# RWKV's 16x16 block inverses turned by one transpose on TensorE in place of a DRAM round trip, one state step for both head pairs, and a new order of the mixers' work

## The chip, the cores and the metric

The kernel runs on one core of a Trainium2 chip. Its time is the device time of one execution in microseconds (us), as the median of several executions. The engines of the core are named as the profile names them: PE (TensorE, matmuls; PEld is its weight load), DVE (VectorE), ACT (ScalarE), POOL (GpSimd), SP (SyncE, which here only issues DMAs, in order).

## What is computed

Two decoder layers on 256 positions of 1024 channels. In each, one input projection feeds three token mixers (RetNet retention, FoX forgetting attention, RWKV-7), whose outputs are projected, merged under sigmoid gates, projected again and added to x; a SwiGLU network follows.

```python
for l in range(DEPTH):                      # 2
    h = _rmsnorm(x, mix_norm[l])
    ret_c, fox_c, rwkv_c, gate_c = jnp.split(h @ w_in[l], splits, axis=-1)
    y_ret, y_fox, y_rwkv = ...              # three mixers, 4 heads of 64 each
    merged = (gates[:, :, 0] * (y_ret @ p_ret[l]) + gates[:, :, 1] * (y_fox @ p_fox[l])
              + gates[:, :, 2] * (y_rwkv @ p_rwkv[l]))
    x = x + merged @ w_out[l]
    g, u = jnp.split(_rmsnorm(x, ffn_norm[l]) @ w_gate_up[l], 2, axis=-1)
    x = x + (jax.nn.silu(g) * u) @ w_down[l]

def step(state, inp):                       # RWKV-7, per head, over 256 positions
    r_t, w_t, k_t, v_t, a_t, b_t = inp
    sa = jnp.einsum('bhvk,bhk->bhv', state, a_t)
    state = (state * w_t[:, :, None, :] + sa[..., None] * b_t[:, :, None, :]
             + v_t[..., None] * k_t[:, :, None, :])
    return state, jnp.einsum('bhvk,bhk->bhv', state, r_t)
```

## The kernel before

The weights stream from DRAM through SP's queue in loads of mostly 1 MB (`raw`, L294). ACT rounds each half to `whi` (L304), DVE makes the rest `wlo` (L305), and PE multiplies with hi*hi, lo*hi and hi*lo, three matmuls (L321, L324, L325) of 128x256 for one f32 product. These weight matmuls (tiles `mm`, `mv`, `mqk`) are nearly all of PE's work, and everything of the mixers stands between them in small groups.

RWKV is computed in four chunks of C = 64 positions (NC = 4) for four heads, as two pairs `a` of two heads `h`. With `q` the chunk, there are NP = 8 pairs of chunk and head pair, each with two heads on the two halves of the 128 partitions. In the order of the program:

- `pgm` (L844): products of the chunk's vectors, masked into `gg` (L846). Among them is the strictly triangular 64x64 matrix whose inverse is wanted.
- `d1` (L856): its 16x16 diagonal blocks are written to DRAM by 8 DMAs; `lt` (L859) reads them back, one block to a partition (128 blocks), in two DMAs. `nn` (L868) is the part of the matrix off these blocks.
- `ptr` (L879), `pm` (L896): transposes and a product needed later.
- The loop (L903, L905): 15 steps on DVE, each a multiply (`ttmp`) and a reduction into `ti`, invert all 128 blocks at once, a block to a partition.
- `d2`: two DMAs (L909, `d<-ti` in the profile) write `ti` to DRAM, and eight (L914, `tb<-d`) read the blocks back as rows into the block-diagonal places of `tb`.
- `dn` (L919) transposes `tb` by two halves on DVE. `pn1` (L924) multiplies `nn` by `dn`, ACT copies the result to `vn`, `pn2` (L931) multiplies `vn` by `tb`; an addition (L935) gives inverses of the 32x32 blocks, `t1` (L936) transposes two of them. `px1` (L943) and `px2` (L951) make the block between them.
- `pu` (L961), `par` (L972), `pU` (L984), `py` (L993): with the inverse in `tb`, the chunks' products. Then the state goes from chunk to chunk: `pS` (L1003) and `S` (L1008), for each pair `a` by itself, and the rest of `py` (L1018). `pv` (L1036) turns the result for its projection.

FoX has logits `pl` (L1134), `exp` on ACT (L1139), the scaling by the reciprocal sum on DVE (L1143) and transposes `px` (L1147); retention has `psc`, `pyr`, and its normalization `pnr` (L431, sums per head) and `pvr` (L440, spread of the factors).

The mixers are generators. The numbers in `PACE` say how much time a part counts for when the next generator is chosen (the one with the least on its clock), and how far a piece of it is put ahead (`hp_...`); the framework's scheduler then sets each engine's order by priority and readiness. SP's order follows from the same, and a queue serves strictly in order.

## Time and profile before

| | us |
|---|---|
| median of 3 runs | 784.35 (783.7 to 785.01) |
| the profiled execution | 785.53 |
| its span | 783.5 |
| PE busy in it | 772.7 |
| DVE busy | 570.4 |
| ACT busy | 405.0 |
| POOL busy | 18.7 |

The profile shows one execution. The span goes from its first to its last instruction. Mixers of layer 0 lie at about 30 to 180 us, the feed-forward network of layer 0 at 228 to 410, and the mixers of layer 1 at 410 to 570. A row of a timeline is start and duration in us, engine, line, operation, output<-inputs, and in brackets the idle time before it with what ended it. A small f32 matmul has two records, and the duration of a matmul is its latency: the time from the start of one to the start of the next is what it takes of PE. "PEclk" is the clock that the throttle granted, with 1.00 for full.

### The profile page before, as it was taken

Reading aid. Unit: us, or ns where it says so; the run is one execution under the profiler, and the core shown is the slowest. Engines: PE = TensorE matmul, PEld = TensorE weight load, DVE = VectorE, ACT = ScalarE, POOL = GpSimd, SP = SyncE. Lnnn points to the kernel's source line nnn. Section 1 sums busy time; section 2 is a strip of 40 time slices with the busy share of each in tenths; the row PEclk is TensorE's granted clock in tenths of the full one; section 3 lists DMA queues with packets and bytes.
Section 4 is the critical chain, followed back from the end, with each engine's and each line's share of the span. In section 5 each row is a group of like instructions: output and inputs, shape, how many; then the busy total and the mean of one; then the engine's idle time right before and its main releaser. Section 6 shows DMA issues by size and latency. Waiting matters only on the chain.

```text
span 783.5 us, 16496 instructions
## 1 busy us (share of the span) xinstructions
PE 772.7 (99%) x7001; PEld 754.8 (96%) x7001; DVE 570.4 (73%) x902; ACT 405.0 (52%) x562; POOL 18.7 (2%) x53
## 2 busy tenths in 40 slices
PE   8999999999999999999999999998999999999998
PEld 7999999999999999999998999997999999999998
DVE  6987988869866666655668798976788776666442
ACT  5777445445555445444447773543456554544331
POOL 4000000010000000000020000000000000000000
PEclk9999999999999999999999999999999999999999
DMA  9646434335555555556464454444265465455650
GB/s 341 246 175 197 157 129 166 116 130 215 190 203 173 204 199 182 198 178 206 170 219 169 179 180 148 141 146 136 97 216 200 161 216 201 179 212 166 212 189 28
DMA packets 28378, 140.42 MB, mean 179 GB/s; under 512 B 7664, under 2 KB 9232, under 8 KB 13456
## 3 DMA queue, kind: packets, MB, share of 16 engines
q1 hardware_dynamic: 27872, 138.58, 50.7%
q8 instruction: 55, 0.90, 0.5%
q10 hardware_dynamic: 432, 0.79, 0.4%
q14 instruction: 19, 0.16, 0.1%
HBM read 136.97 MB, written 1.33 MB: 177 GB/s over the span
## 4 chain that ended last, share of the span: by engine, by line
PE 95%; DMA 2%; DVE 1%; ACT 1%; SPq 0%; issue 0%; ACTq 0%; DVEq 0%
PE mm L325 26%; PE mm L321 26%; PE mm L324 26%; PE mm L382 3%; PE mv L515 1%; PE mv L517 1%; PE mv L516 1%; PE mqk L517 1%; PE mqk L516 1%; PE mqk L515 1%; DMA raw<-in_win 1%; PE pl L1134 1%; DMA d<-ti 1%; PE px L1147 0%; PE pu L961 0%; PE ptr L879 0%
## 5 line engine op out<-in xcount | busy, mean ns | idle before, releaser
L304 ACT CAST whi<-raw 128x1024 fp32r<-128x1024 f32 (+3 forms) x258 | 264.7, 1030 | 295.1 <-PE mm L324 209.2
L305 DVE TENSOR_TENSOR wlo<-raw,whi 128x1024 fp32r<-128x1024 f32 (+3 forms) x258 | 308.6, 1198 | 134.2 <-ACT whi L304 133.4
L321 PE MATMUL mm<-xh,whi 128*128 128x256 f32 x1248 | 347.8, 279 | 0.0
L324 PE MATMUL mm<-xl,whi 128*128 128x256 f32 x1200 | 333.5, 278 | 0.0
L325 PE MATMUL mm<-xh,wlo 128*128 128x256 f32 x1200 | 333.3, 278 | 0.0
L321 PEld LDWEIGHTS mm<-xh,whi 128*128 128x128 f32 x1248 | 234.6, 188 | 0.4
L324 PEld LDWEIGHTS mm<-xl,whi 128*128 128x128 f32 x1200 | 225.4, 188 | 0.8 <-issue 0.5
L325 PEld LDWEIGHTS mm<-xh,wlo 128*128 128x128 f32 x1200 | 225.3, 188 | 0.9 <-issue 0.5
L325 PE MATMUL mm<-hi,wlo 128*128 128x256 f32 x576 | 160.0, 278 | 0.0
L324 PE MATMUL mm<-lo,whi 128*128 128x256 f32 x576 | 159.7, 277 | 0.2
L321 PE MATMUL mm<-hi,whi 128*128 128x256 f32 x576 | 159.5, 277 | 0.0
L324 PEld LDWEIGHTS mm<-lo,whi 128*128 128x128 f32 x576 | 108.4, 188 | 0.6 <-DVE lo L449 0.6
L325 PEld LDWEIGHTS mm<-hi,wlo 128*128 128x128 f32 x576 | 108.4, 188 | 0.3
L321 PEld LDWEIGHTS mm<-hi,whi 128*128 128x128 f32 x576 | 108.5, 188 | 0.0
L685 DVE TENSOR_TENSOR h<-t,mm 128x512 f32<-128x512 f32 x22 | 15.1, 686 | 9.9 <-PE mm L325 8.4
L679 DVE TENSOR_TENSOR t<-mm,rstd 128x512 f32<-128x512 f32 (+1 forms) x24 | 15.1, 644 | 7.9 <-PE mm L325 7.9
L515 PE MATMUL mv<-whi,xh 128*128 128x260 f32 (+1 forms) x64 | 18.8, 293 | 0.0
L517 PE MATMUL mv<-whi,xl 128*128 128x260 f32 (+1 forms) x64 | 18.4, 287 | 0.0
L516 PE MATMUL mv<-wlo,xh 128*128 128x260 f32 (+1 forms) x64 | 18.0, 281 | 0.0
L620 ACT ACTIVATE gate<-gate 128x512 f32<-128x512 f32 x24 | 15.1, 629 | 5.6 <-DVE gate L619 5.6
L619 DVE TENSOR_TENSOR gate<-mm,rstd 128x512 f32<-128x512 f32 x24 | 16.4, 684 | 1.1 <-PE mm L325 1.0
L628 DVE SCALAR_TENSOR_TENSOR gate<-gate,mm 128x512 f32<-128x512 f32 x24 | 15.8, 678 | 0.1
(263 smaller groups left out, 742.7 us busy)
## 6 DMA issues: line engine op xcount, KB each, us to landing
raw<-in_wg SPq DMA_DIRECT2D x44, 1024.0 KB
raw<-in_wgate SPq DMA_DIRECT2D x24, 1024.0 KB
raw<-in_wd SPq DMA_DIRECT2D x16, 1024.0 KB
raw<-in_win SPq DMA_DIRECT2D x12, 1024.0 KB
raw<-in_wo SPq DMA_DIRECT2D x8, 1024.0 KB
raw<-in_wd SPq DMA_DIRECT2D x8, 768.0 KB
raw<-in_wqk SPq DMA_DIRECT2D x4, 1024.0 KB
raw<-in_pp SPq DMA_DIRECT2D x4, 1024.0 KB
```

What stands on the lines that cost most here:

```text
L304: nc.scalar.copy(hi[:, :m * width], r)
L305: nc.vector.tensor_tensor(out=lo[:, :m * width], in0=r, in1=hi[:, :m * width].bitcast(F32), op=ALU.subtract)
L321: nc.tensor.matmul(out, wh, xh, start=first, stop=False)
L324: nc.tensor.matmul(out, wh, xl, start=False, stop=False)
L325: nc.tensor.matmul(out, wl, xh, start=False, stop=last)
L382: self.nc.tensor.matmul(ps[j][:, m, :], ws[b][i], xs[k][o], start=n == b == kk == 0, stop=n == 2 and b == 3 and kk == 3)
L515: nc.tensor.matmul(out, xh[:, s], wh, start=first, stop=False)
L516: nc.tensor.matmul(out, xh[:, s], wl, start=False, stop=False)
L517: nc.tensor.matmul(out, xl[:, s], wh, start=False, stop=last)
L619: nc.vector.tensor_tensor(out=g, in0=ps, in1=self.b2(rstd), op=ALU.mult)
L620: nc.scalar.activation(g, g, AF.Tanh, scale=0.5)
L628: nc.vector.scalar_tensor_tensor(out=g, in0=g, scalar=1.0, in1=ps, op0=ALU.add, op1=ALU.mult)
```

## The change

- `ti` has another layout: partition u*16+q holds row q of the eight blocks of chunk-and-pair u, with the blocks in the free dimension. `lt` must then hold each of the u's eight blocks on all its 16 partitions: one DMA reads 64 KB from DRAM sixteen times into 1 MB. It takes the buffer of `rav` (tag q8), so it also waits until PE has read `rav`.
- `d2` and its ten DMAs a layer are gone. One 128x128 transpose on PE (`pti`) puts the blocks' columns on the right partitions; one multiply on DVE with a constant mask (`odd`) spreads them to block-diagonal 32x32 windows (`dn`), and one stream transpose (`tw`) turns those. `pn1` has 32 columns in place of 64, `pn2` is 32 matmuls of 32x32 in place of 16 of 64x64, the addition works on `tw` at once, and ACT copies `tw` into `tb` in four pieces.
- The state step is one for both pairs: one `pS` tile of four matmuls and one addition per chunk.
- FoX's scaling by `rc` moves from DVE to ACT.
- `PACE` has new numbers, and `PINS` names 15 groups of matmuls that keep the order in which the program issues them.

```diff
+PINS = {"pU", "par", "pc", "pgm", "pl", "pm", "pn1", "pn2", "pnk", "pqk", "psc", "pss", "px1", "py", "pyf"}
-PACE = {... 'hp_merge': 44.0, 'hp_turn': 0.0, ... 'rwkv9': 15.39, ... 'rwkv23': 25.79, ...}
+PACE = {... 'hp_merge': 100.0, 'hp_turn': 68, ... 'rwkv9': 13.22, ... 'rwkv23': 12.06, ...}
-    d["tinit"] = ((p[:, None, None] // 64) * 8 + np.arange(8)[None, :, None] == np.arange(Q)[None, None, :]).astype(f)
+    d["tinit"] = np.broadcast_to(p[:, None, None] % Q == np.arange(Q)[None, None, :], (P, 8, Q)).astype(f)
+    d["odd"] = (p[:, None] // Q % 2 == np.arange(2)[None, :]).astype(f)
...
+    def pinned(self, ins):
+        if self.pend in PINS:
+            self.tc.keep_in_program_order(ins)
+        self.pend = None
+        return ins
...
-                nc.sync.dma_start(d1[b, h].rearrange("u s t -> s u t"), gg[64 * h + o:64 * h + o + Q, h::2, 2 * C + o:2 * C + o + Q])
-        lt = big.tile([P, Q, Q], F32, name="lt")
-        for g4 in range(2):
-            nc.sync.dma_start(lt[g4 * 64:(g4 + 1) * 64].rearrange("p s t -> p (s t)"), d1.rearrange("b h u s t -> (b h u) (s t)"))
+                nc.sync.dma_start(d1[:, 4 * h + b].rearrange("u s t -> s u t"), gg[64 * h + o:64 * h + o + Q, h::2, 2 * C + o:2 * C + o + Q])
+        lt = big.tile([P, 8, Q, Q], F32, tag="q8", bufs=1, name=self.nm("lt"))
+        ltf = lt.rearrange("p b s t -> p b (s t)")
+        nc.sync.dma_start(ltf.rearrange("p b x -> p (b x)"),
+                          d1.rearrange("u b s t -> u (b s t)").unsqueeze(1).broadcast_to([NP, Q, 8 * Q * Q]))
...
-        for g4 in range(2):
-            nc.sync.dma_start(d2.rearrange("b h u c j -> (b h u) c j")[:, g4 * 8:(g4 + 1) * 8, :].rearrange("q c j -> q (c j)"),
-                              ti[g4 * 64:(g4 + 1) * 64].rearrange("p c j -> p (c j)"))
-        for h in range(2):
-            for b in range(4):
-                o = b * Q
-                nc.sync.dma_start(tb[64 * h + o:64 * h + o + Q, :, h, o:o + Q], d2[b, h].rearrange("u c j -> c u j"))
...
+        px = self.ps.tile([P, NP, Q], F32, tag="sm", bufs=SM, name=self.nm("pti"))
+        self.trans(px.rearrange("p u c -> p (u c)"), ti.rearrange("p b j -> p (b j)"), idn)
+        dn = self.t2.tile([P, NP, B], F32, tag="t2", name=self.nm("dn"))
+        nc.vector.tensor_tensor(out=dn.rearrange("p u (e c) -> p u e c", e=2), in0=px.unsqueeze(2).broadcast_to([P, NP, 2, Q]),
+                                in1=c["odd"].unsqueeze(1).unsqueeze(3).broadcast_to([P, NP, 2, Q]), op=ALU.mult)
+        tw = self.t2.tile([P, NP, B], F32, tag="t2", name=self.nm("tw"))
+        nc.vector.transpose(tw, dn)
...
-            for h in range(2):
-                nc.tensor.matmul(px[hs[h], p, :], vn[hs[h], p, :], tb[hs[h], p, h, :], start=True, stop=True, tile_position=(64 * h, 64 * h))
+            for w in range(4):
+                self.mmul(px[win[w], p, :], vn[win[w], p, :], tw[win[w], p, :], start=True, stop=True, tile_position=(w * B, w * B))
...
-        for h in range(2):
-            nc.vector.tensor_tensor(out=tb[hs[h], :, h, :], in0=tb[hs[h], :, h, :], in1=px[hs[h]], op=ALU.add)
-            nc.vector.transpose(t1[lo[h]], tb[lo[h], :, h, 0:B])
+        nc.vector.tensor_tensor(out=tw, in0=tw, in1=px, op=ALU.add)
+        nc.vector.transpose(t1, tw)
+        for w in range(4):
+            o = w % 2 * B
+            nc.scalar.copy(tb[win[w], :, w // 2, o:o + B], tw[win[w]])
...
         for q in range(1, NC - 1):
+            pS = self.ps.tile([P, 2, 64], F32, tag="sm", bufs=SM, name=self.nm("pS"))
             for a in range(2):
-                pS = self.ps.tile([P, 64], F32, tag="sm", bufs=SM, name=self.nm("pS"))
...
-                ns = sm.tile([P, 64], F32, tag="S", bufs=2 * NC - 4, name=self.nm("S"))
-                nc.vector.tensor_tensor(out=ns, in0=us[:, a, q, :], in1=pS, op=ALU.add)
+            ns = sm.tile([P, 2, 64], F32, tag="S", bufs=NC - 2, name=self.nm("S"))
+            nc.vector.tensor_tensor(out=ns, in0=us[:, :, q, :], in1=pS, op=ALU.add)
...
-                nc.vector.tensor_scalar(out=lg[:, h, 0:n], in0=lg[:, h, 0:n], scalar1=rc[:, h:h + 1], scalar2=None, op0=ALU.mult)
+                nc.scalar.activation(lg[:, h, 0:n], lg[:, h, 0:n], AF.Copy, scale=rc[:, h:h + 1])
```

How the instructions stand in a row on an engine, at three places of layer 0. First SP's queue from the blocks' way out to the loads behind the inverse, before (`in_pp` and `in_wgate` are weights; x8 says eight alike):

```order
L856 DMA d_0_1325<-gg 16x8x16 x8
L294 DMA raw_1629<-in_wgate 128x2048
L859 DMA lt<-d_0_1325 64x256 x2
L294 DMA raw_1691<-in_pp 128x2048
L294 DMA raw_1856<-in_pp 128x2048
L294 DMA raw_1978<-in_wgate 128x2048
L294 DMA raw_2109<-in_wgate 128x2048
L909 DMA d_0_1326<-ti 64x128 x2
L914 DMA tb_1341<-d_0_1326 16x8x16 x8
L294 DMA raw_2197<-in_wgate 128x2048
```

and in the changed kernel:

```order
L877 DMA d_0_1325<-gg 16x8x16 x8
L880 DMA lt_1334<-d_0_1325 128x1x2048
L309 DMA raw_1613<-in_wgate 128x2048
L309 DMA raw_1738<-in_pp 128x2048
L309 DMA raw_1800<-in_pp 128x2048
L309 DMA raw_2005<-in_wgate 128x2048
L309 DMA raw_2136<-in_wgate 128x2048
L309 DMA raw_2220<-in_wgate 128x2048
```

The load of `lt` stands ahead of the weight load that it followed, and nothing stands between the weight loads at the end. Second DVE from the gates ahead of `dn` on, before (`gate` are the merge's gates, L619 and L628, and their lines move to L634 and L643):

```order
L628 SCALAR_TENSOR_TENSOR gate_1429<-gate_1429,mm_1977 128x512
L919 STREAM_TRANSPOSE dn_1783<-tb_1341 64x512
L628 SCALAR_TENSOR_TENSOR gate_1509<-gate_1509,mm_1997 128x512
L305 TENSOR_TENSOR wlo_2031<-raw_1978,whi_2030 128x1024
L919 STREAM_TRANSPOSE dn_1783<-tb_1341 64x512
L628 SCALAR_TENSOR_TENSOR gate_1597<-gate_1597,mm_2029 128x512
L628 SCALAR_TENSOR_TENSOR gate_1659<-gate_1659,mm_2048 128x512
L630 TENSOR_TENSOR gate_1201<-gate_1201,gate_1597 128x512
L630 TENSOR_TENSOR gate_1322<-gate_1322,gate_1659 128x512
L305 TENSOR_TENSOR wlo_2112<-raw_2109,whi_2111 128x1024
L935 TENSOR_TENSOR tb_1341<-tb_1341,pn_264_1834 64x8x64 x2
L936 STREAM_TRANSPOSE t_265_1851<-tb_1341 32x256 x2
```

and in the changed kernel:

```order
L320 TENSOR_TENSOR wlo_1773<-raw_1738,whi_1772 128x1024
L320 TENSOR_TENSOR wlo_1803<-raw_1800,whi_1802 128x1024
L634 TENSOR_TENSOR gate_1830<-mm_1771,rstd_434 128x512
L937 TENSOR_TENSOR dn_1835<-pti_1833,con 128x256
L320 TENSOR_TENSOR wlo_1974<-raw_1800,whi_1973 128x1024
L940 STREAM_TRANSPOSE tw_1837<-dn_1835 128x256
L643 SCALAR_TENSOR_TENSOR gate_1164<-gate_1164,mm_1972 128x512
L960 TENSOR_TENSOR tw_1837<-tw_1837,pn_271_1858 128x256
L961 STREAM_TRANSPOSE t_272_1891<-tw_1837 128x256
```

One `dn` stands where two stood with a gate and a split between, and one addition and one transpose where there were two each. Third PE around `pn1` and `pn2`, before:

```order
L324 MATMUL mm_2108<-lo_1235,whi_1929 128x256
L924 MATMUL pn_259_1786<-dn_1783,nn_1343 64x64 x16
L325 MATMUL mm_2108<-hi_1234,wlo_1930 128x256
L321 MATMUL mm_2108<-hi_1234,whi_1929 128x256
L324 MATMUL mm_2108<-lo_1235,whi_1929 128x256
L325 MATMUL mm_2108<-hi_1234,wlo_1930 128x256
L321 MATMUL mm_2108<-hi_1234,whi_1929 128x256
L324 MATMUL mm_2108<-lo_1235,whi_1929 128x256
L931 MATMUL pn_264_1834<-tb_1341,vn_1803 64x64 x16
L325 MATMUL mm_2108<-hi_1234,wlo_1930 128x256
```

and in the changed kernel (all PE lines are now those of the two wrappers, L234 for matmuls and L237 for transposes):

```order
L237 MATMUL pti_1833<-con,ti 128x128
L234 MATMUL mm_1972<-hi_1734,whi_1740 128x256
L234 MATMUL mm_1972<-lo_1735,whi_1740 128x256
L234 MATMUL mm_1972<-hi_1734,wlo_1741 128x256
L234 MATMUL mm_1972<-hi_1734,whi_1740 128x256
L234 MATMUL mm_1972<-lo_1735,whi_1740 128x256
L234 MATMUL mm_1972<-hi_1734,wlo_1741 128x256
L234 MATMUL mm_1972<-hi_1734,whi_1740 128x256
L234 MATMUL mm_1972<-lo_1735,whi_1740 128x256
L234 MATMUL mm_1972<-hi_1734,wlo_1741 128x256
L234 MATMUL mm_1972<-hi_1734,whi_1740 128x256
L234 MATMUL pn_269_1839<-dn_1835,nn_1341 64x32 x16
```

`pti` now stands ten weight matmuls ahead of `pn1`; before, `pn1` had no work of its own chain on PE ahead of it, and waited for the DMAs and DVE alone. Behind this piece seven weight matmuls follow up to `pn2`, where there were six, and nine up to `px1`, where there were 22.

More of the change, by code (lines that the diff above doesn't have):

```diff
@@ L514, in mm3n @@
         (wh, wl), (xh, xl) = w, x
[L515 to L517 removed]
+        self.mmul(out, xh[:, s], wh, start=first, stop=False)
+        self.mmul(out, xh[:, s], wl, start=False, stop=False)
+        self.mmul(out, xl[:, s], wh, start=False, stop=last)
     def gemm_n(self, width, xs, name="mv"):
```

140 lines of the change are left out of this document (84 added, 56 removed).

## Prediction

> **What bounds the kernel now.** I read the page's busy shares first, then busy time stage by stage, then PE's list of waits, and then the timelines around the longest of them.
>
> ```profile
> PE 772.7 (99%) x7001; PEld 754.8 (96%) x7001; DVE 570.4 (73%) x902; ACT 405.0 (52%) x562; POOL 18.7 (2%) x53
> ```
> ```profile
> core 0: us, PE busy (x) PEld busy (x) DVE busy (x) ACT busy (x) POOL busy (x), PEclk, DMA share, GB/s
> 30.00:180.00 150.00, 148.56 (x1436) 140.66 (x1435) 127.06 (x248) 85.27 (x139) 3.27 (x10) 1.00 0.45 153
> 410.00:570.00 160.00, 156.56 (x1491) 148.57 (x1490) 131.81 (x254) 88.77 (x144) 1.30 (x4) 0.99 0.45 152
> ```
>
> TensorE (PE) bounds the kernel. The two rows are the mixers of layers 0 and 1, where alone the edit works: PE idles there 150 - 148.56 = 1.44 us and 160 - 156.56 = 3.44 us. So 4.9 us, less than 1% of the time, is all that waits can give back; the rest can come only from PE's own work and from its clock, 0.99 in layer 1. DVE (85% and 82% busy) is the next engine. PE's list of waits says where the idle time lies:
>
> ```profile
> PE pn L924 <- DVE dn L919: 2.8, 2, 2.4
> PE px L1147 <- DVE lg L1143: 0.7, 2, 0.4
> ```
>
> The first row is the very place of the edit: of two waits, 2.8 us together, one is 2.4. Here is how that one comes about, on SP's queue and then on DVE:
>
> ```profile
> 518.75 0.33 SPq L294 DMA_DIRECT2D raw<-in_wgate  x1
> 519.13 1.13 SPq L909 DMA_DIRECT2D d<-ti  x2
> 524.62 4.91 SPq L914 DMA_DIRECT2D tb<-d  x8
> 529.63 0.38 SPq L294 DMA_DIRECT2D raw<-in_wgate  x1
> ```
> ```profile
> 529.34 0.70 DVE L919 STREAM_TRANSPOSE dn<-tb 64x512 f32<-64x512 f32 x1 [1.98 <-DMA tb<-d]
> 529.98 0.64 DVE L628 SCALAR_TENSOR_TENSOR gate<-gate,mm 128x512 f32<-128x512 f32 x1
> 530.55 1.20 DVE L305 TENSOR_TENSOR wlo<-raw,whi 128x1024 fp32r<-128x1024 f32 x1
> 531.78 0.71 DVE L919 STREAM_TRANSPOSE dn<-tb 64x512 f32<-64x512 f32 x1
> ```
>
> In layer 1 the write of `ti` (d<-ti, 519.13) was issued right behind a 1 MB weight load; the eight reads (tb<-d) began at 524.62, and the first `dn` waited for them until 529.34. A gate and a weight split stand between it and the second `dn` on DVE, and only after that does pn1 (L924) start. PE's own rows, layer 1 and then layer 0, show a second loss behind the wait:
>
> ```profile
> 532.55 1.31 PE L924 MATMUL pn<-dn,nn 64*64 64x64 f32 x32 [2.40 <-DVE dn L919]
> 535.36 1.78 PE L931 MATMUL pn<-tb,vn 64*64 64x64 f32 x32
> 537.07 0.39 PE L325 MATMUL mm<-hi,wlo 128*128 128x256 f32 x1
> ...
> 145.87 1.15 PE L924 MATMUL pn<-dn,nn 64*64 64x64 f32 x32 [0.41 <-DVE dn L919]
> 147.85 1.24 PE L931 MATMUL pn<-tb,vn 64*64 64x64 f32 x32
> 149.03 0.38 PE L325 MATMUL mm<-hi,wlo 128*128 128x256 f32 x1
> ...
> 151.81 0.69 PE L943 MATMUL px<-t,gg 32*32 32x32 f32 x32
> 152.43 0.39 PE L321 MATMUL mm<-xh,whi 128*128 128x256 f32 x1
> ```
> ```profile
> 533.00:534.00 1.00, 1.00 (x25) 0.88 (x22) 1.00 (x3) 0.10 (x1) 0.00 (x0) 0.69 0.96 397
> 534.00:535.00 1.00, 1.00 (x5) 1.00 (x6) 1.00 (x3) 0.48 (x1) 0.00 (x0) 0.50 0.96 352
> ```
>
> The same stretch, pn1, six weight matmuls and pn2, took 537.07 - 532.55 = 4.52 us in layer 1 and 149.03 - 145.87 = 3.16 in layer 0: 1.36 us more, at a granted clock that fell to 0.50 after a wait of 2.40 us and did not fall after one of 0.41.
>
> **The change, part by part** (both layers, against the profiled execution: 785.53 us, span 783.5).
>
> *Inverses by PE.* `ti` no longer goes to DRAM and back: 2 writes and 8 reads a layer leave SP's queue, and the loads behind them move up by that. In their place stand one 128x128 transpose on PE (pti), 10 weight matmuls, and pn1; the mask multiply `dn` on DVE needs only to fit into those ten. At the pitch that layer 0 shows (pn1 and pn2 apart 1.98 us, six matmuls .90 of it, hence .11 to .12 each beside the turn) ten give 1.14 us. On DVE one gate (0.64) stands ahead of `dn`, whose 128x256 is half of what the 0.71 row handles, some 0.4. It fits by about a tenth of a microsecond; I take a wait of 0.15 each. The 2.40 falls by 2.25 and the 0.41 by 0.26. The wait is then far under 2.40, so I count the clock's 1.36 back as well. Together -3.9. Between the last step of the DVE loop and pti lie about 8 us by the new order (from pgm to pti 252 weight matmuls and the groups between them, some 34 us, of which d1 and lt take about 12, the loop's 30 steps with the splits between them 13 to 14), so `ti` is ready in time.
>
> *pn1, pn2, tw, tb.* pn1's matmuls have 32 columns for 64: its 1.08 us (145.87 to the next row, 146.95 by the six at .90) lies between that and the .62 of 32x32 in the px row; I take .9, -0.4 for two layers. pn2 becomes 32 small matmuls, 64 records at the px row's .62/32 = 19 ns, 1.24 for 1.18: +0.1. `tw` is added once (128x256) instead of in two 64x512 halves and transposed once: DVE is relieved by about a microsecond a layer, which it gives to nobody at once. ACT gets four copies from `tw` to `tb`; px1 and px2 do not need them, and pu stands behind both, so they cost nothing unless px1 and px2 come early. ACT idles 65 of 150 us and is the cover.
>
> *pti and more turns.* The new order splits pnr and pvr into four single matmuls each and pl and the px transposes of fox into more pieces: 12 more excursions a layer from the weight stream. What does one cost?
>
> ```profile
> 75.18 0.43 PE L1147 MATMUL px<-con,lg 128*128 128x128 f32 x2
> 75.37 0.37 PE L517 MATMUL mv<-whi,xl 128*128 128x256 f32 x1
> 75.57 0.43 PE L1147 MATMUL px<-con,lg 128*128 128x128 f32 x2
> ...
> 103.86 1.09 PE L879 MATMUL ptr<-con,rav 128*128 128x128 f32 x8
> 104.70 0.36 PE L325 MATMUL mm<-xh,wlo 128*128 128x256 f32 x1
> ...
> 162.60 0.33 PE L1003 MATMUL pS<-S,ar 64*64 64x64 f32 x4
> 162.87 0.38 PE L325 MATMUL mm<-xh,wlo 128*128 128x256 f32 x1
> 163.67 0.38 PE L325 MATMUL mm<-xh,wlo 128*128 128x256 f32 x1
> 163.99 0.34 PE L1018 MATMUL py<-S,ar 64*64 64x64 f32 x8
> ```
>
> In a row of eight a transpose takes .84/8 = .105 us; alone between weight matmuls .19, and the weight matmul after it .20 for .115. So a full-height single costs up to .17 over its work, and nothing if its group paid for the turn anyway, as pnr's four may. Between 0 and .17 I take .08, since half of the twelve are parts of groups that already stood alone: 12 x 2 x .08 = +1.9, and pti itself .19 + .085 twice, +0.5.
>
> *States of both pairs in one step.* pS and py make three groups where there were five; a half-height group between single weight matmuls costs more: the matmul ahead of py above took .32 for .115, and the group of pS .27 for four half-size ones. I take .27 a group: 2 x 2 x .27 = -1.1. Two additions on DVE fewer; the waits of pS on S were shorter than the weight matmuls between and are longer covered now (21 and 8 matmuls for 3 and 1).
>
> *fox.* The scaling by `rc` moves from DVE to ACT. The second row of waits (0.7 in two) shrinks where the new order puts 61 weight matmuls for 49 ahead: -0.5; a like wait of the merge for `lo` goes (-0.2).
>
> *lt.* One broadcast of 1 MB replaces two loads of 64 KB, and stands ahead of the weight load that it followed.
>
> ```profile
> 104.53 4.58 SPq L856 DMA_DIRECT2D d<-gg  x8
> 109.51 0.35 SPq L294 DMA_DIRECT2D raw<-in_wgate  x1
> 110.35 1.14 SPq L859 DMA_DIRECT2D lt<-d  x2
> 114.64 7.65 SPq L294 DMA_DIRECT2D raw<-in_pp  x2
> ...
> 115.16 0.13 POOL L860 MEMSET lt<- 128x16 f32 x1 [28.25 <-DMA lt<-d]
> ```
> ```profile
> 118.00:120.00 2.00, 2.00 (x20) 2.00 (x19) 1.93 (x7) 1.88 (x4) 0.00 (x0) 1.00 0.41 168
> 120.00:122.00 2.00, 2.00 (x20) 2.00 (x19) 2.00 (x4) 1.17 (x2) 0.00 (x0) 1.00 0.04 8
> ```
>
> Before, lt was there 115.16 - 110.35 = 4.8 us after issue, behind a 1 MB load. A 1 MB load issued at 114.64 had moved its bytes by 120 (168 GB/s, then 8): at most 5.4 us. So the new lt is late by at most .6, and the splits queued behind the loop's first step on DVE have about 5 us before PE wants them. I cost it at nothing between -0 and +0.3.
> [...]
>
> *New waits.* With DVE as full as it is, each layer has four tight places: px1 behind the add and transpose, px2 behind v1, pu behind tb, pS behind us. Each is between 0 and the .41 that layer 0 had at pn1; I take .1: 2 x 4 x .1 = +0.8.
>
> Sum: -3.9 - 0.3 + 1.9 + 0.5 - 1.1 - 0.7 + 0.8 = -2.8, from 785.53 to 782.7 for a profiled execution. That one lies 1.18 above the median of the runs, 784.35, which spread over 1.3 us; I carry the difference over: 781.5. The turns are the softest term, and their likelier error is downward: if the singles of one group cost no more than in it, 1.9 becomes 0 and the median 779.6. For that I set 781.2.
>
> **Rivals.** (a) *New waits take the place of the old.* For it: `dn` fits by a tenth, DVE serves in order, and a gate or a split (1.20) that slips ahead delays px1 too. Against: layer 0 had the same engines as full and lost .41 in all. At .4 for each of eight places, +2.4 more: 783.6, the same by measurement.
> (b) *The turns cost what the rows' upper end says*, .17 and, where a wait adds, .3: 24 x .3 = 7.2 for 1.9, hence 786.5, slower. It decides from about .2 a turn. Against: singles in the rows show .17 at most.
> (c) *lt is late.* 128 partitions read 8 KB each out of the same 64 KB; if that takes 12 us, about 1 to 2 us of wait on a split reach PE in each layer, and after a long wait the clock's 1.36: +5, 786. It decides from about 11 us after issue; the 168 GB/s row speaks against.
> (d) *The dip of the clock is not the wait's.* If PE's clock falls on too little work over a fixed stretch, a wait of 2.40 us alone is not enough and pn1 and pn2, small matmuls, share the blame; then 1.36 stays: 782.6. Against: layer 0 ran the same groups at full clock. [...]
> (e) *The change does less than it says*: layer 1's stall grew in the profiled execution and is smaller in the timed runs; the runs then lack the 1.18 already and gain that much less: 784.35 - (2.8 - 1.18) = 782.7.
>
> **How the numbers follow.** This kernel's runs can tell 0.2%, 1.57 us, from no change: faster is under 782.78, slower over 785.92. The forecast 781.2 has .54, its own range 778.4 to 782.7; (a) .14, same; (b) .07 and (c) .06, slower; (d) .08, faster; (e) .11, half of it the same. Faster .54 + .08 + .05 = .67; same .14 + .06 = .20; slower .13. The low end has all 4.9 us of idle time and the clock's 1.36 gone, with turns and new work at nothing: 784.35 - 6.3 = 778.1. The high end takes in (a) and stops where (b) and (c) begin, 785.0.
>
> **What the profile after will show.** Right: pn1 waits under .3 us in both layers, the clock is 1.00 through layer 1's mixers, no d<-ti or tb<-d on SP's queue, lt lands within 5.5 us of issue, PE idle in each mixer stage under 1.5 us. The turns: pnr's and pvr's singles with the next weight matmul at .20 each or at .115. Wrong: a wait of PE at px1, px2 or pu over .4, POOL's lt memset 8 us or more after issue with a split waiting behind the loop, or a clock under 1.00 with no wait ahead of it.

## The result, and the profile after

The changed kernel is slower: a median of 795.5 us (793.62 to 797.1, four runs) against 784.68 (783.7 to 785.43) of the kernel before on the same chip, a ratio of 1.0141 [1.0127, 1.0156]. The prediction had 781.2 us with a range of 778.1 to 785.0. The profiled execution took 793.62, its span is 791.8 (before: 785.53 and 783.5).

The busy shares first, then the mixers of layers 0 and 1, stage by stage (columns as in the prediction):

```profile
PE 774.3 (98%) x7067; PEld 758.0 (96%) x7067; DVE 562.1 (71%) x878; ACT 413.6 (52%) x586; POOL 19.0 (2%) x53
```
```profile
30.00:180.00 150.00, 144.61 (x1423) 137.69 (x1422) 119.28 (x233) 86.89 (x148) 3.37 (x10) 0.98 0.48 152
410.00:570.00 160.00, 153.87 (x1494) 146.37 (x1493) 124.32 (x243) 90.49 (x152) 1.50 (x4) 0.98 0.47 150
```

PE idles 5.39 us and 6.13 us there, where it idled 1.44 and 3.44, and the granted clock is 0.98 in both. The list of waits of PE, and one row of that of DVE, name new places:

```profile
PE mm L234 <- DVE wlo L320: 6.0, 2, 3.5
PE pn L234 <- DVE dn L937: 4.5, 2, 3.1
```
```profile
DVE ttmp L927 <- POOL lt L882: 20.1, 2, 10.5
```

PE now waits for a weight split (`wlo`), and for `dn` longer than before. DVE itself stands 10 us in each layer at the first step of the loop (`ttmp`), for `lt`. SP's queue and POOL in layer 0 say how late `lt` is:

```profile
101.59 3.66 SPq L877 DMA_DIRECT2D d<-gg  x8
107.77 0.69 SPq L880 DMA_DIRECT2D lt<-d  x1
109.60 0.36 SPq L309 DMA_DIRECT2D raw<-in_wgate  x1
```
```profile
123.01 0.32 POOL L882 MEMSET lt<- 128x128 f32 x1 [34.36 <-PE mm L234]
```

POOL's memset of the diagonal starts when `lt` has landed: 123.01 - 107.77 = 15.2 us after its issue (14.7 in layer 1: 497.31 and 511.98), where the prediction had at most 5.4. (The bracket names a matmul; the same row of layer 1 has `[33.35 <-DMA lt<-d]` there.) From there the lateness runs over DVE to PE, in layer 0:

```profile
123.36 0.18 DVE L927 TENSOR_TENSOR ttmp<-ti,lt 128x16 f32<-128x16 f32 x1 [10.54 <-POOL lt L882]
...
126.53 0.22 DVE L928 TENSOR_REDUCE ti<-ttmp 128x8 f32<-128x64 f32 x1
126.67 1.21 DVE L320 TENSOR_TENSOR wlo<-raw,whi 128x1024 fp32r<-128x1024 f32 x1
127.80 0.28 DVE L927 TENSOR_TENSOR ttmp<-ti,lt 128x72 f32<-128x72 f32 x1
```
```profile
127.94 0.58 PE L234 MATMUL mm<-xh,wlo 128*128 128x256 f32 x1 [3.47 <-DVE wlo L320]
...
144.85 1.12 PE L234 MATMUL pn<-dn,nn 64*64 64x32 f32 x32 [1.47 <-DVE dn L937]
```
```profile
516.92 0.38 PE L234 MATMUL mm<-xh,wlo 128*128 128x256 f32 x1 [2.48 <-DVE wlo L320]
...
533.85 1.92 PE L234 MATMUL pn<-dn,nn 64*64 64x32 f32 x32 [3.06 <-DVE dn L937]
```

A split that has nothing to do with `lt` stands behind the first seven steps of the loop in DVE's order, so it starts at 126.67, and PE has no weights until 127.94. What the loop still lacks at its end shows once more at pn1. In this execution the clock then halves behind the longer of the two waits of each layer (the last section says why not behind the other):

```profile
128.00:129.00 1.00, 1.00 (x5) 1.00 (x6) 0.90 (x5) 0.00 (x0) 0.00 (x0) 0.50 0.02 8
...
133.00:134.00 1.00, 1.00 (x8) 1.00 (x7) 1.00 (x2) 0.00 (x0) 0.00 (x0) 0.65 1.06 451
```
```profile
534.00:536.00 2.00, 2.00 (x33) 1.94 (x34) 1.28 (x2) 0.31 (x2) 0.00 (x0) 0.50 0.88 315
...
538.00:540.00 2.00, 2.00 (x51) 1.94 (x41) 0.87 (x2) 0.83 (x3) 0.00 (x0) 0.53 0.53 213
```

It is 0.50 from PE's return at 127.94 to about 133.7, and from 533.85 to about 539.9: by that clock half of 5.8 and 6.0 us is lost, 5.9 in all (a weight matmul starts every .21 us at 539.09 and every .11 at 539.93). The experiment e1 below is this kernel with `lt` in time and has a span of 774.5: of the 17.3 us between them, 10.7 are idle time of PE in these two stages (5.39 + 6.13 against .43 + .44) and 5.9 the clock.

### The profile page after: what moved, and what is told of

Same layout as the page of the kernel before. It is cut to its first block, busy times and chain, and to the rows that moved or that the text cites. A ratio compares the mean times of both kernels' runs of the same rounds, so it can differ in the third digit from the quotient of the medians.

```text
span 791.8 us, 16588 instructions
## 1 busy us (share of the span) xinstructions
PE 774.3 (98%) x7067; PEld 758.0 (96%) x7067; DVE 562.1 (71%) x878; ACT 413.6 (52%) x586; POOL 19.0 (2%) x53
## 4 chain that ended last, share of the span: by engine, by line
PE 91%; DVE 5%; DMA 3%; ACT 1%; issue 1%; POOL 0%; ACTq 0%; POOLq 0%
PE mm L234 77%; PE mv L234 3%; PE mqk L234 3%; DMA lt<-d 2%; DVE wlo L320 2%; DVE ttmp L927 1%; DMA raw<-in_win 1%; PE pl L234 1%; PE pn L234 1%; DVE ti L928 1%; DVE gate L634 1%; PE pgm L234 1%; PE py L234 0%; PE par L234 0%; PE psc L234 0%
## 5 line engine op out<-in xcount | busy, mean ns | idle before, releaser
L234 PE MATMUL mm<-xh,wlo 128*128 128x256 f32 x1312 | 357.9, 279 | 6.1 <-DVE wlo L320 6.0
L234 PE MATMUL mm<-xh,whi 128*128 128x256 f32 x1312 | 360.2, 280 | 1.6 <-DVE xh L480 1.1
L234 PE MATMUL mm<-xl,whi 128*128 128x256 f32 x1312 | 357.3, 278 | 0.0
L234 PEld LDWEIGHTS mm<-xh,wlo 128*128 128x128 f32 x1312 | 244.1, 189 | 6.8 <-DVE wlo L320 6.7
L234 PEld LDWEIGHTS mm<-xh,whi 128*128 128x128 f32 x1312 | 244.3, 189 | 2.6 <-ACT whi L319 2.1
L234 PEld LDWEIGHTS mm<-xl,whi 128*128 128x128 f32 x1312 | 244.1, 189 | 0.2
L234 PE MATMUL mm<-hi,wlo 128*128 128x256 f32 x576 | 160.8, 279 | 0.0
L234 PE MATMUL mm<-hi,whi 128*128 128x256 f32 x576 | 160.7, 279 | 0.0
L234 PE MATMUL mm<-lo,whi 128*128 128x256 f32 x576 | 160.4, 278 | 0.2 <-DVE lo L464 0.2
L234 PEld LDWEIGHTS mm<-lo,whi 128*128 128x128 f32 x576 | 108.8, 189 | 0.5 <-DVE lo L464 0.4
L234 PEld LDWEIGHTS mm<-hi,wlo 128*128 128x128 f32 x576 | 108.7, 189 | 0.4
L234 PEld LDWEIGHTS mm<-hi,whi 128*128 128x128 f32 x576 | 108.8, 189 | 0.3
L643 DVE SCALAR_TENSOR_TENSOR gate<-gate,mm 128x512 f32<-128x512 f32 x24 | 16.4, 685 | 10.8 <-PE mm L234 10.4
L927 DVE TENSOR_TENSOR ttmp<-ti,lt 128x16 f32<-128x16 f32 (+14 forms) x30 | 8.5, 283 | 20.5 <-POOL lt L882 20.1
L234 PE MATMUL mv<-whi,xh 128*128 128x260 f32 (+1 forms) x64 | 18.6, 290 | 0.0
L234 PE MATMUL mv<-whi,xl 128*128 128x260 f32 (+1 forms) x64 | 18.5, 290 | 0.0
L234 PE MATMUL mv<-wlo,xh 128*128 128x260 f32 (+1 forms) x64 | 18.2, 284 | 0.0
```

Source lines behind the costliest of these rows:

```text
L234: return self.pinned(self.nc.tensor.matmul(*a, **k))
L643: nc.vector.scalar_tensor_tensor(out=g, in0=g, scalar=1.0, in1=ps, op0=ALU.add, op1=ALU.mult)
L927: nc.vector.tensor_tensor(out=tmp[:, :, 0:n], in0=ti[:, :, 0:n], in1=lt[:, :, 0:n, i], op=ALU.mult)
```

## Experiments

Five groups of kernels ran; each has its own runs of the kernel before beside it, with medians of 785.21 (e1 to e3), 783.97 (e4 to e7), 784.75 (e8 to e11), 784.36 (e12 to e14) and 784.91 (e15, e16). The first question: is it `lt`, and is it slow because 64 KB just written to DRAM are read sixteen times (the prediction's rival c), or for another reason?

**e1: `lt` filled from 1 MB of other bytes.** Everything else stays, in the same order and behind the same writes of `d1`.

```diff
-        nc.sync.dma_start(ltf..., d1.rearrange("u b s t -> u (b s t)").unsqueeze(1).broadcast_to([NP, Q, 8 * Q * Q]))
+        lw = nc.sync.dma_start(ltf..., self.d["wg"][l, 0, 0])        # 128x2048 of a weight, after all writes of d1
```

> The changed kernel with one edit: lt's 1 MB is loaded from 1 MB of a weight, every byte read once, behind the same eight d1 writes and with the same order of instructions on every engine. Its values are then not the blocks of the matrix (the result of RWKV is meaningless; the work is the same). Theory A (lt is slow because 16 partitions read the same 64 KB): its pieces of 8 KB take 0.31 us as those of other loads, not 0.6 to 0.95; lt is there about 5 us after issue, not 15; PE's waits for wlo (6.0 us) and for dn (4.5) fall to under 0.5 in all; time 781 to 784 us. Theory B (lt shares the DMA engines with the 1 MB load issued 2 us behind it, whatever it reads): the pieces stay at 0.6 to 0.95 us and the time at 794 to 797.

Measured: 776.26 us, ratio 0.9894 [0.9879, 0.9908]. The mixers' stages, and `lt` on SP's queue and on POOL:

```profile
30.00:180.00 150.00, 149.57 (x1492) 142.92 (x1490) 125.50 (x240) 91.60 (x153) 3.38 (x10) 1.00 0.47 163
410.00:570.00 160.00, 159.56 (x1581) 152.94 (x1580) 133.66 (x249) 97.76 (x159) 1.49 (x4) 1.00 0.48 169
```
```profile
107.92 0.36 SPq L882 DMA_DIRECT2D lt<-in_wg  x1
112.90 0.32 POOL L885 MEMSET lt<- 128x128 f32 x1 [24.22 <-DMA lt<-in_wg]
```

`lt` is there after 5.0 us, PE idles .43 and .44 us, the clock is 1.00, and no wait for `wlo` or `dn` is left. So all of the loss hangs on this one transfer, and without it the change gains 8.95 us, nearly three times what the prediction had; the time is 5 us below the range that I gave for this run, because the rest of the change is worth more than I took it for.

**e1b: the same weights, but 64 KB of them read sixteen times.** Its source keeps the form of the changed kernel's, eight rows outside, sixteen repeats inside.

```diff
+        lw = nc.sync.dma_start(ltf..., self.d["wg"][l, 0, 0][0:NP].unsqueeze(1).broadcast_to([NP, Q, 8 * Q * Q]))
```

> The same edit, but lt reads 64 KB of a weight sixteen times over (values again meaningless). Theory A (same addresses): slow as in the changed kernel, pieces of 0.6 to 0.95 us, lt 13 to 16 us after issue, 793 to 797 us. Theory C (DRAM that was written a moment ago is slow to read): as quick as a load of distinct bytes, 5 us, 781 to 784.

Measured (one run): 794.95 us, `lt` 15.0 us after issue. So `lt` is as late without bytes that have just been written. e1 and e1b differ in two things, though: in the re-reading and in the form.

**e2: partition q*8+u for u*16+q.** The sixteen repeats stand outside, the eight rows inside; the transpose's columns are read in the other order. It computes the same as the changed kernel.

```diff
-    ... p[:, None, None] % Q == ...
+    ... p[:, None, None] // 8 == ...                                  # tinit
-        d1.rearrange("u b s t -> u (b s t)").unsqueeze(1).broadcast_to([NP, Q, 8 * Q * Q])
+        d1.rearrange("u b s t -> u (b s t)").unsqueeze(0).broadcast_to([Q, NP, 8 * Q * Q])
-        px = self.ps.tile([P, NP, Q], ...)
+        px = self.ps.tile([P, Q, NP], ...).rearrange("p c u -> p u c")   # pti
```

> The changed kernel with the partitions in the other order, q*8+u for u*16+q (the constant, the broadcast and the reading of pti turned accordingly): neighbouring partitions read different 8 KB of the 64. Same instructions in the same order. Theory A, if the DMA engines take the partitions in turn: eight different addresses at a time for one, pieces at 0.3 to 0.5 us, lt in 6 to 9 us, 783 to 788 us. Theory A, if each engine takes eight neighbours: now all start on the same address where before they spread over eight, lt as late or later, 794 to 800. Theory B: no change, 794 to 797.

Measured: 776.71 us, ratio 0.9899 [0.9884, 0.9913].

```profile
30.00:180.00 150.00, 149.04 (x1486) 142.32 (x1486) 124.61 (x239) 90.78 (x153) 3.39 (x10) 1.00 0.48 163
410.00:570.00 160.00, 159.55 (x1579) 152.86 (x1579) 133.22 (x249) 97.16 (x160) 1.50 (x4) 1.00 0.49 169
```
```profile
108.48 0.60 SPq L880 DMA_DIRECT2D lt<-d  x1
115.60 0.33 POOL L882 MEMSET lt<- 128x128 f32 x1 [26.85 <-DMA lt<-d]
```

The same bytes are read as often, and are there after 7.1 us for 15.2. The time is again below the ranges that I gave. This version beats both kernels.

**e3: the loop's first step kept behind the DVE work that stands ahead of it in the program**, so that `wlo` needn't wait for it.

```diff
+            if i == 1:
+                self.tc.keep_in_program_order(first)        # the first ttmp
```

> The changed kernel with the first step of the loop on DVE pinned behind what the program issues ahead of it: three splits (wlo) and two gates move ahead of the loop, pti comes 28 weight matmuls later. lt itself stays slow (13 to 16 us from issue to landing). If its lateness costs by holding the splits behind it in DVE's order, PE's wait for wlo (6.0 us) and most of that for dn (4.5) go, the clock stays at 1.00, and the time is 782 to 786 us. If instead the many turns or new waits of the order cost the time, 792 or more.

Measured: 793.38 us, ratio 1.0113 [1.0093, 1.0134]; `lt` after 14.5 us. My expectation missed. The wait for `wlo` is gone from the list of PE's waits, and this stands at its head:

```profile
PE pti L237 <- DVE ti L930: 10.4, 2, 5.9
```

The same lateness, 10.4 us in two waits for 6.0 + 4.5 in four, reaches PE at the transpose. Where DVE is blocked matters little: the loop is then too late for `pti`.

**e4: the weight load that follows `lt` held back until `lt` has landed**, to see `lt` alone on the DMA engines.

```diff
-                nc.sync.dma_start(raw[:, :n * width], src)
+                ld = nc.sync.dma_start(raw[:, :n * width], src)
+                ...                                          # the load behind lt's: wait for lt's completion
+                self.tc.add_manual_dep(ld.ins, self.held[0].ins.name, ...)
```

> The changed kernel (lt as it is, each 8 KB read by 16 neighbouring partitions), but the weight load behind lt on SP's queue is issued only when lt has landed. Same order of instructions on every engine. If half of lt's lateness comes from this load, whose pieces take turns with lt's on the DMA engines and are slowed with them: lt's 128 pieces alone, at 0.6 to 0.95 us on 16 engines, need 5 to 7.6 us and lt lands 7 to 10 us after issue instead of 14.5; PE's waits fall under 1 us a layer; 776.5 to 781 us. If the pieces are slow only because two loads run at once: 0.31 us, lt in 5 us, 776 to 777. If the other load does not matter: lt in 13 us or more, 791 to 796.

Measured: 790.54 us, ratio 1.0071 [1.0054, 1.0088]. Both the time of `lt` and its cost were larger than I expected for this case. The DMA engines over the same stretch, e4 and then the changed kernel (last two columns: mean busy share of the sixteen, GB/s):

```profile
110.00:118.00 8.00, 8.00 (x73) 8.00 (x72) 2.77 (x3) 3.81 (x5) 0.00 (x0) 1.00 0.52 120
```
```profile
110.00:118.00 8.00, 8.00 (x73) 8.00 (x72) 2.82 (x3) 3.81 (x5) 0.00 (x0) 1.00 0.95 164
```

Alone, `lt` takes 11.9 us (107.75 to 119.62) and keeps about half of the engines busy (0.52). In the changed kernel the next load fills the others, so that the share looks full at 164 GB/s, and `lt` takes 3 us more. At 11.9 us the price is still 13.8 us against e2, in waits for `dn` (6.1 us in two) and the clock behind them.

**e5, e8, e9: fewer rows read, more repeats outside** (e2 with 2 rows x 64, 1 row x 128 and 4 rows x 32).

```diff
-        .unsqueeze(0).broadcast_to([Q, NP, 8 * Q * Q])
+        [0:4].unsqueeze(0).broadcast_to([P // 4, 4, 8 * Q * Q])      # e9; e5 with 2 rows, e8 with [0:1] on all 128
```

> The version with partitions in the order q*8+u, but the broadcast repeats only the first two of the eight 8 KB rows, in turn (values of RWKV are then meaningless; work and order are the same). If what counts is how many different addresses the engines read at a time: with two, pieces of 0.7 to 0.95 us, lt 12 to 15 us after issue as in the changed kernel, 788 to 796 us. If it is enough that neighbours differ: pieces of 0.4 to 0.65 us, lt in 7 us, 776 to 778.

> The version with partitions q*8+u, but all 128 partitions read the same 8 KB (values of RWKV meaningless; same work and order). So far: sixteen neighbours on the same 8 KB, 14.5 us from issue to landing; eight in turn 7.1; two in turn 5.2. If repeated neighbours are the slow thing, one address for all is at least as slow as the changed kernel: 14 us or more, 792 us or more. If it is how many engines meet on one address, the same or worse still. If neither (5 to 7 us, 776 to 777), then the slowness belongs to the pattern of the changed kernel and not to reading an address again.

> As before with four of the eight 8 KB rows in turn. Between two (5.2 us) and eight in turn (7.1 us) if the number matters in a regular way: 5 to 7.2 us, 776 to 777.5 us.

Measured, one run each: 776.24, 776.24 and 775.57 us; `lt` after 5.2, 4.8 and 5.4 us. When 128 partitions read one and the same 8 KB row the load is as fast as one of 1 MB of different bytes (5.0). Re-reading by itself costs nothing here.

**e12, e13: rows 9 KB apart in DRAM for 8**, in e2 and in the changed kernel.

```diff
-        d1 = self.dr.tile([NP, 8, Q, Q], F32, name=f"d1_{l}")
+        d1 = self.dr.tile([NP, 9, Q, Q], F32, name=f"d1_{l}")[:, 0:8]
```

> The version with partitions q*8+u, with the eight rows of 8 KB in DRAM 9 KB apart instead of 8. Its lt took 7.1 us from issue to landing with pieces of 0.43 to 0.65 us, where four rows in turn, two, one, or 128 distinct took 4.7 to 5.4 us at 0.31. If the pieces are slow because eight rows at a distance of 8 KB get in each other's way where the memory is read: pieces of 0.31 us, lt in 5 us, PE's wait for dn (0.5) gone, 775.5 to 776.6 us. If it is the number eight: no change, 776.4 to 777.0.

> The changed kernel (partitions u*16+q) with rows 9 KB apart. With the load behind it held back, its 128 pieces ran at a DMA share of 0.52, eight at a time, at 0.51 to 0.65 us. If both the half of the engines and slow pieces made lt late: the pieces go to 0.31 us, eight engines do 16 each, which with the load behind in turn gives 9 to 11 us from issue to landing for 14.5; 777 to 787 us. If only the pieces' slowness counts (the share is a result of it): 5 us, 776. If the distance has no part in it: 14.5 us, 793 to 797.

Measured: 776.52 us, 0.9903 [0.9889, 0.9917], `lt` 7.6; and 793.2 us, 1.0117 [1.0103, 1.0132], `lt` 14.7. The distance plays no visible part either.

**e14: the changed kernel's form with 4 rows outside and 32 repeats inside.**

```diff
-        .unsqueeze(1).broadcast_to([NP, Q, 8 * Q * Q])
+        [0:4].unsqueeze(1).broadcast_to([4, 32, 8 * Q * Q])
```

> The changed kernel, but the broadcast gives each of only four rows to 32 neighbouring partitions (values of RWKV meaningless; same work and order). Four rows in turn had pieces of 0.31 us and were spread over all engines. If the outermost dimension of the broadcast (here 4, in the changed kernel 8, in the turned one 16) is what the pieces are spread over: four engines, 32 pieces each, in turn with the load behind, lt 14 to 18 us after issue and a DMA share of about 0.25 ahead of that load; 792 to 800 us. If the spread is even: 5 us, 775.5 to 776.5.

Measured (one run): 808.02 us, `lt` after 22.6 us, both beyond what I expected. The DMA engines at the end of `lt`, and the list of PE's waits:

```profile
126.00:128.00 2.00, 0.00 (x0) 0.00 (x0) 0.00 (x0) 0.00 (x0) 0.00 (x0) 0.89 0.25 70
```
```profile
PE mm L234 <- DVE wlo L320: 21.4, 2, 10.8
```

The share, 0.25, is that of four engines of sixteen, for four rows outside, as it was that of eight (0.52) for eight in e4.

**e15, e16: distinct bytes, as in e1, in the forms 16x8 and 8x16.** Nothing is read twice.

```diff
+        lw = nc.sync.dma_start(ltf..., self.d["wg"][l, 0, 0].rearrange("(j i) x -> i j x", i=Q))     # e15; i=NP in e16
```

> The load of 1 MB of distinct bytes (e1) with its source rows taken in another order, so that the transfer has dimensions of 16 and 8 for one of 128: partition 8i+j reads row 16j+i of a weight (values of RWKV meaningless; same work and order). No byte is read twice. Theory D (the shape of the transfer decides: the outermost dimension is dealt to the engines, and engines that take eight neighbouring partitions each meet in pairs on the way into SBUF): pieces of 0.5 to 0.65 us as in the version with q*8+u, lt 6.5 to 7.5 us after issue, 776.3 to 777. Theory A' (reading eight rows again and again makes the pieces slow): 0.31 us, 5 us.

> The same with dimensions of 8 and 16, as in the changed kernel: partition 16i+j reads row 8j+i, no byte twice. Theory D: eight engines do it, pieces of 0.5 to 0.95 us, lt 13 to 16 us after issue, 792 to 797 us as in the changed kernel, although nothing is read twice. Theory A': 5 to 9 us, 776 to 782.

Measured (one run each): 776.27 us with `lt` after 7.4 us, and 795.61 us with `lt` after 14.9 us. These are e2 and the changed kernel again, without a byte read twice. The DMA share and rate while `lt` is under way, e1, e15 and e16:

```profile
110.00:112.00 2.00, 2.00 (x20) 2.00 (x19) 2.00 (x4) 1.20 (x2) 0.00 (x0) 1.00 0.98 414
```
```profile
110.00:112.00 2.00, 2.00 (x20) 2.00 (x18) 2.00 (x3) 1.52 (x3) 0.00 (x0) 1.00 0.96 209
```
```profile
116.00:118.00 2.00, 2.00 (x20) 2.00 (x19) 0.00 (x0) 0.62 (x1) 0.00 (x0) 1.00 1.02 147
```

All runs of the 1 MB into `lt` by its form (outermost dimension x next), from issue to landing in layer 0:

| form | what is read | us |
|---|---|---|
| 4x32 | e14, 4 rows | 22.6 |
| 8x16 | changed kernel 15.2; e3 14.5; e13 14.7; e1b weights again 15.0; e16 distinct 14.9; e4 with no load behind | 14.5 to 15.2; 11.9 |
| 16x8 | e2 7.1; e12 7.6; e15 distinct 7.4 | 7.1 to 7.6 |
| 32x4, 64x2 | e9 5.4; e5 5.2 | 5.2 to 5.4 |
| 128 | e1 distinct 5.0; e8 one row 4.8 | 4.8 to 5.0 |

The second question: what are the other parts worth?

**e10: the kernel before with the new `PACE` and `PINS` alone.** Inverses through DRAM, states of each pair and fox's scaling on DVE as before.

```diff
+PINS = {"pU", "par", ...}                       # as after
-PACE = {'hp_piece': 4.0, ...}
+PACE = {'fox6': 1.54, ...}                      # as after
```

> The kernel before with nothing but the new PACE numbers and PINS: inverses through DRAM, states pair by pair, FoX's scaling on DVE. With the state step of both pairs and the scaling on ACT it took 778.0 us. If the order by itself took out the waits and the slow clock: 778 to 780.5. If the two small edits carry a part of it: 781 to 784, with waits of PE at FoX's px or pS on S.

Measured: 781.15 us, ratio 0.9954 [0.9938, 0.9971].

```profile
30.00:180.00 150.00, 148.95 (x1440) 141.65 (x1439) 127.27 (x248) 85.87 (x139) 3.50 (x10) 1.00 0.45 153
410.00:570.00 160.00, 158.89 (x1526) 151.68 (x1526) 135.63 (x259) 91.44 (x145) 1.30 (x4) 1.00 0.46 158
```

The wait for `dn` is gone and the clock is 1.00, with `ti` still going through DRAM. The order alone brings that. In layer 1 the reads of `tb` now begin 3.6 us behind the write of `ti` (508.14 and 511.78), for 5.5 before (519.13 and 524.62), and from 518.50 the two `dn` run back to back, with no gate and no split between them. How much each of the two is worth was not measured.

**e6: the changed kernel with the inverses through DRAM** (`lt` small, `d2`, `tb` and 64-column pn1 as before; states of both pairs and fox's scaling on ACT as after).

```diff
-        lt = big.tile([P, 8, Q, Q], F32, tag="q8", bufs=1, name=self.nm("lt"))
+        lt = big.tile([P, Q, Q], F32, name="lt")
...
+                nc.sync.dma_start(tb[64 * h + o:64 * h + o + Q, :, h, o:o + Q], d2[b, h].rearrange("u c j -> c u j"))
-        self.trans(px.rearrange("p u c -> p (u c)"), ti.rearrange("p b j -> p (b j)"), idn)
```

> The changed kernel with the block inverses' part undone: small lt, ti written to DRAM and read back as rows, two dn, pn1 and pn2 on 64x64, as before; the new PACE and PINS, the state step of both pairs and FoX's scaling on ACT stay. It says what the new order and the two small edits are worth without the inverses by PE. With the version of partitions q*8+u at 776.7 us: pn2 back at 1.17 us and pn1 at 1.08 cost 0.5 a layer, the wait at pn1 0.4 to 2.4 with the slow clock behind the long one. If the inverses' part is most of the gain: 782 to 786. If the order is most of it: 777 to 781.

Measured: 777.97 us, ratio 0.9916 [0.9901, 0.9930]. Its distance to e2, 1.3 us, is what the inverses by PE bring with their `lt` in a good form; the two ran in different groups and their intervals overlap, so it is not clear of noise.

**e7: e2 with the old `PACE` and no pins.**

```diff
-PINS = {"pU", "par", ...}
+PINS = set()
-PACE = {'fox6': 1.54, ...}
+PACE = {'hp_piece': 4.0, ...}                   # as before
```

> The version with partitions q*8+u (inverses by PE, state step of both pairs, scaling on ACT), but with the PACE numbers of the kernel before and nothing pinned. If the new order is worth little beside the inverses: 776 to 778.5 us. If it is what took most of the time out: 780 to 786, with PE's time between the projections spread over more turns or with waits at pn1, px1 or px of FoX.

Measured: 788.74 us (783.88 to 790.27, ten runs), ratio 1.005 [1.0032, 1.0068], more than either range that I gave. PE's waits begin with these:

```profile
PE pti L237 <- DVE ti L928: 3.2, 1, 3.2
PE pti L237 <- issue: 2.1, 1, 2.1
```

In the old order the loop isn't done when `pti` comes. The second row names no releaser, but DVE's last step of the loop ends at 525.28 there and `pti` starts at 525.38. The inverses by PE bring nothing without the new order.

**e11: e2 with fox's scaling on DVE**, as before the change.

```diff
-                nc.scalar.activation(lg[:, h, 0:n], lg[:, h, 0:n], AF.Copy, scale=rc[:, h:h + 1])
+                nc.vector.tensor_scalar(out=lg[:, h, 0:n], in0=lg[:, h, 0:n], scalar1=rc[:, h:h + 1], scalar2=None, op0=ALU.mult)
```

> The version with partitions q*8+u (776.7 us), with FoX's scaling back on DVE. The scaling costs DVE 2.5 us a layer in a stretch where PE has 51 to 61 weight matmuls of cover. If the cover is enough: 776.5 to 777.5. If px waits for it as before (0.7 in two waits, and a loop on DVE that starts later): 777.5 to 779.

Measured: 778.84 us (778.34 to 779.85), ratio 0.9928 [0.9913, 0.9943], 2.1 us more than e2, which ran in another group; the intervals touch. PE waits again for `lg`, and for `rsc` of the retention:

```profile
PE px L237 <- DVE lg L1183: 0.7, 2, 0.3
PE pyr L234 <- DVE rsc L1271: 0.5, 2, 0.3
```

## Why the prediction was wrong, by its steps

**The step that failed: `lt`, "I cost it at nothing between -0 and +0.3".** It measured +19.2 us (795.5 against e1's 776.26). The estimate took 5.4 us from a 1 MB load of 128 rows and applied it to a 1 MB load of another form. Both move as many bytes, but `lt` has eight rows outside and sixteen repeats inside, and in these runs the busy share of the DMA engines goes with the outermost dimension, not with the bytes: .25 for 4 at the end of `lt` (e14), .52 for 8 with `lt` alone (e4), .96 for 16 (e15) and .98 for 128 (e1) with the next load already queued behind it. The order rows in front of the prediction showed that form (128x1x2048) as one DMA and hid the 8 x 16; the diff had it, in `unsqueeze(1).broadcast_to([NP, Q, ...])`.

The number of engines is not all: 16x8 also fills sixteen, and yet takes 7.1 to 7.6 us at 209 GB/s where 128 rows take 5.0 at 414. Worked out from share and rate of e15 and e1, a piece of 8 KB (8192 bytes) takes 16 x .96 x 8192 / 209,000 = .60 us there and 16 x .98 x 8192 / 414,000 = .31 in e1. Why this form has slower pieces is left open, and no run shows the meeting in pairs that theory D of e15 names; re-reading and fresh writes (e15) and the distance in DRAM (e12) are excluded.

**Rival (c) came true in its effect, with its place right, its price too small and its reason wrong.** It had the wait on a split, from about 11 us on, at +5 us. The place is `wlo` in PE's first row of waits, and the prediction's own sign of being wrong, POOL's memset of `lt` 8 us or more after issue with a split behind the loop, is what the profile shows. e4 bounds the point: at 11.9 us the loss is already 13.8 us against e2, at 7.1 us next to nothing. The price was too small for two reasons. The lateness of the loop reaches PE at more than one place (6.0 us at `wlo` and 4.5 at `dn`, or 10.4 at `pti` in e3), and the halved clock costs about 3 us in each layer, not 1.36 in one. The reason of (c), that all partitions read the same 64 KB, is refuted (e8, e16); that it still named the lateness was luck. The row of 168 GB/s that spoke against (c) is of a load of 128 distinct rows, and says nothing of re-reading or of the form.

**"Inverses by PE, -3.9": size right, cause wrong.** pn1's wait and the clock's dip do go (e1, e2: idle .4 to 1.0 us a stage, clock 1.00). But e10 gets rid of both with the new order alone, for -3.6 us in all, while the inverses by PE add about 1.3 (e6 to e2) and bring nothing in the old order (e7). The prediction credited the end of the round trip through DRAM; what sufficed was the new order around it.

**Rivals (d) and (e).** (d) is half right: the clock does fall on idle time inside a fixed stretch, here a step of 3.41 us (last section). But the wait of 2.40 us was enough for it, and the 1.36 us went with the wait (e10). (e) has a point too. In the seven runs of the kernel before that stand beside e1 to e3, two have a granted clock of 1.00 and take 783.39 and 783.56 us; five have .998 and take 784.81 to 785.63. So the dip is not in every run.

**The turns, "+1.9": measured at nothing for pnr and pvr.** Here is pnr on PE, as one group of four before and the first two of its four singles in e2, and then pti:

```profile
108.44 0.95 PE L431 MATMUL pnr<-con,rsq 128*128 128x2 f32 x8
109.25 0.36 PE L321 MATMUL mm<-xh,whi 128*128 128x256 f32 x1
109.46 0.28 PE L324 MATMUL mm<-xl,whi 128*128 128x256 f32 x1
```
```profile
111.99 0.28 PE L234 MATMUL pnr<-con,rsq 128*128 128x2 f32 x2
112.13 0.36 PE L234 MATMUL mm<-xh,wlo 128*128 128x256 f32 x1
112.33 0.28 PE L234 MATMUL pnr<-con,rsq 128*128 128x2 f32 x2
...
135.45 0.28 PE L234 MATMUL mm<-xh,wlo 128*128 128x256 f32 x1
135.56 0.27 PE L237 MATMUL pti<-con,ti 128*128 128x128 f32 x1
135.59 0.37 PE L234 MATMUL mm<-hi,whi 128*128 128x256 f32 x1
135.79 0.28 PE L234 MATMUL mm<-lo,whi 128*128 128x256 f32 x1
```

The group with the weight matmul behind it takes 109.46 - 108.44 = 1.02 us, .905 without that matmul's .115. A single and a weight matmul take 112.33 - 111.99 = .34, .225 without it, four times which is .90. A single costs what it cost in its group, the case that the prediction named as the likelier error. pvr's four singles in e2 take .46 us beside their weight matmuls, for .49 in the group before. The new pieces of fox's pl and px were not priced. pti takes 135.79 - 135.45 - .23 = .11, for .275.

**pn2, "+0.1": -1.0 for two layers.** The row that I priced it by, px, works on two tiles; pn2 now works on four. In e2, pn1 and pn2:

```profile
137.51 1.12 PE L234 MATMUL pn<-dn,nn 64*64 64x32 f32 x32 [0.52 <-DVE dn L938]
138.56 0.38 PE L234 MATMUL mm<-lo,whi 128*128 128x256 f32 x1
...
139.58 0.75 PE L234 MATMUL pn<-tw,vn 32*32 32x32 f32 x64
140.26 0.38 PE L234 MATMUL mm<-hi,wlo 128*128 128x256 f32 x1
```

64 records take .68 us, 10.6 ns each, for the 19 of px and the 1.18 us of the old pn2. pn1 takes 1.05 for 1.08: of the "-0.4" for its fewer columns, next to nothing came.

**fox, "-0.7": about 2.1** (e11 against e2). In the profiled executions, 778.34 and 776.93, the distance is 1.4 us, and the two rows of waits in e11 make up 1.2; the timed runs of e11 spread over 1.5 us. **States in one step, "-1.1"**: e10 to e6 is -3.2 us, less fox's 2.1 leaves 1.1, an agreement by difference only. **New waits, "+0.8"**: about nothing once `lt` is in time; e2 has one of .5 us at `dn`, and e1 none.

With `lt` harmless the change gains 8.5 (e2) to 9.0 us (e1), where the forecast had 2.8: turns and pti 2.2, pn2 and pn1 .8, fox 1.4 and the new waits .8 make 5.2 of the 5.7 to 6.2 between them. So errors of opposite sign lay in the prediction, and the one that came from a single row of another form decided.

## What to carry to other kernels

Before a DMA is priced by another one of as many bytes, compare the forms: write down the outermost dimension of the side that is read. Here the same 1 MB took 15.2 us with 8 outside, 7.1 with 16 and 5.0 with the 128 partitions, and an exchange of two dimensions in one layout was worth 18.8 us. A new order and a new algorithm in one change want a run of the order alone: here it took away the stall that the algorithm was credited with. And moving the work around a late tensor on one engine gained 2 us of the 19 here (e3); making the tensor earlier gained nearly all (e2).

## What was unexpected of the hardware

- A full DMA share is no full rate: 0.95 to 1.02 at 147 to 164 GB/s in the changed kernel and e16, 0.96 at 209 in e15, 0.98 at 414 in e1.
- The next load slows the one in front of it, although that one leaves half of the engines free (a share of 0.52 in e4): 15.2 us with it, 11.9 without. From 110 to 118 us the two move 164 GB/s together, for 120 of `lt` alone, so the queue issues them in order but does not serve one after the other.
- The length of a wait does not decide whether the clock halves. It fell to 0.50 behind waits of 3.47, 3.06, 2.40 (the kernel before) and 2.08 us (e14), and not behind 2.48 (516.92) and 1.47 us (144.85). What decides in these traces is PE's idle time inside one step of a fixed grid. Every stretch at 0.50 in the mixers begins on a grid of 3.41 us and lasts one to four of its steps: from 126.87 to 133.70 and from 533.06 to 539.89 in the changed kernel, from 533.38 to 536.79 in the kernel before. The two starts in the changed kernel lie 406.19 us apart, which is 119 times 3.413; in e13 two lie 17.07 apart, 5 times. Here are two steps, first in the kernel before and then in the changed one:

```profile
529.97:533.38 3.41, 1.01 (x30) 0.83 (x30) 3.35 (x6) 0.97 (x1) 0.00 (x0) 1.00 0.81 262
```
```profile
512.58:515.99 3.41, 1.86 (x38) 1.46 (x36) 3.34 (x24) 0.94 (x2) 0.00 (x0) 1.00 0.55 223
```

  The wait of 2.40 us lies within one step, PE idles 3.41 - 1.01 = 2.40 us in it, and the clock is halved from 533.38 on. The wait of 2.48 us is divided by the end of a step at 515.99, with 1.55 us idle in one and .93 in the next, and the clock stays at 1.00. Over the nine executions that have such stretches, the least idle step with the clock halved behind it has 2.00 us (e13, from 142.49), the most idle one without has 1.56 (e14, from 520.10). Where the limit lies between them, and what ends a slow stretch, no run shows.
